# Attention heads in pairs on two halves of the matrix array

## The chip, the cores and the metric

One core of a Trainium2 chip runs the whole program: two transformer layers (a mixer with a dense feed-forward, a mixer with a mixture of experts), and then a third block with a state space branch and a dilated attention branch. The metric is the device time of one execution in microseconds (us). The engines are TensorE (PE: matmuls and transposes; PEld: its weight loads), VectorE (DVE), ScalarE (ACT), GpSimd (POOL) and SyncE (SP, which issues most DMAs).

## What is computed

256 tokens of 1024 features, all in float32. The attention kinds that matter here, with `q`, `k`, `v` per head:

```python
# mixer, per layer: 4 stick-breaking heads (64), 8 latent heads (keys 96, values 64), 4 banded heads (64)
z = einsum('bqhd,bkhd->bhqk', q, k) * scale            # stick-breaking
log_1mb = where(strict, log_sigmoid(-z), 0.0)
tail = lax.cumsum(log_1mb, axis=3, reverse=True) - log_1mb
w = where(strict, exp(log_sigmoid(z) + tail), 0.0)
o = einsum('bhqk,bkhd->bqhd', w, v)
...
p = softmax(where(allowed, s, NEG), axis=-1)            # latent and banded heads
o = einsum('bhqk,bkhd->bqhd', p, v)
...
# third block: 8 heads (64) in 3 groups of dilations 1, 4, 16; the groups of a head share one softmax
o = einsum('gbsh,gbshd->bshd', softmax(stack(lses)), stack(outs))
# and 32 state space heads: y_diag + y_off of ssd_chunked
```

## The kernel before

Large products run in three passes (`mm3`, `lin_feat`): weights and activations are split into a rounded part (`whi`, `hhi`) and a rest (`wlo`, `hlo`), ACT casts and DVE subtracts. The heads' own products are plain fp32.

Everything beside the large products is written as generators, called units, each `yield` ending a step. A large product calls `hook()` after each piece, `hook()` calls `tick()`, and `tick()` moves every active unit by one step, then starts at most one of `pending`, as long as the weights of the active units (1 by default) stay within `cap[0]`. `now(u)` starts a unit at once with weight 0. This gives the order in which instructions are written down. A scheduler then orders each engine's instructions by a simulated timeline: of those that are ready, the one written first goes first. So a unit's instruction may wait for a tile or a bank while later ones pass it. The engines run their queues in the order so made and wait on semaphores.

PSUM tiles come from four tags with few banks: `d` 3, `s` 2 (scores, and transposes of q and k), `t` 1 (transposes of weights to be applied, sums), `o` 2 (accumulators of heads). While `alone[0]` is set, `abank` takes `s` and `d`, or `t` and `d`, in turn.

`softmax_head` (L724 to L756) is one latent or banded head of a mixer: two score products `psc` (L727, L728) into one bank, two reductions with the mask on DVE (L731, L733), two exponentials on ACT, the division on DVE (L743 to L745), three transposes `ppt` (L750), a copy `pT` on ACT (L752), two value products (L755, L756) into the head's half of an accumulator (`om`, `oc`). Between these stand `yield`s. A head of 64 features lies in partitions 0 to 63 or 64 to 127 of its operands by its number; a latent head's 96 features always lie in partitions 0 to 95. Values always fill half of the output's partitions, by the head's number.

`stick_heads` does four heads: scores `pz` (L773, L774), Abs, Exp, Ln on ACT, masks on POOL, a second set of products `pz` (L790 to L792), Exp, and values `os` (L803, L804).

`mixer` announces `band_T`, four latent heads, four banded, four latent; then the stick products q, k, v run, and after them the loop that fills time until the latent heads' norm is done:

```python
        alone[0] = True
        if first:
            ada_rate[0] = 1
        cap[0] = 5
        ...
        now(stick())
        while M.hi[1] is None:
            tick()
            ada_steps(4)
```

`ada_steps(4)` writes down four steps of the adaptive scales (`ada_gen`): products of 1 MB weight tiles with a vector on DVE (L525, L527), summed on PE (`pada`). In the first mixer four scales are outstanding, in the second none.

In the third block (`second`) the dilated heads come as `dil_head` (L1547): three score steps (`pasc`, L1556, L1557, with reductions at L1560), a shared maximum, exponentials, the division, three times transposes `papT` (L1580 to L1582), a copy `apT`, and values `pao` (L1592, L1593). The products of q, k, v are computed in two halves of four heads; a half's heads are announced behind it, so half 0's heads run along with half 1's products (`cap` 2), and half 1's with the first products of the state space branch (`cap` 4). `ssd_group` (state space heads) has its products into `py` at L1723 and L1725.

Of the kernel before, what the change touches and what calls it, by code (L numbers as in the profile page):

```python
# [37 lines left out]
class Split:  # L38
    """An activation, features on partitions: per pair of 128-feature chunks a rounded tile and the rest."""
# [23 lines left out]
def tile_hybrid_stack(ctx: ExitStack, tc: tile.TileContext, a, out, stages=STAGES):  # L63
    nc = tc.nc
    P = 128
# [9 lines left out]
    # tag: (bytes per partition, slots)  # L75
# [64 lines left out]
    # work that feeds later products lets a norm on the way of the next one pass  # L140
# [8 lines left out]
    def tick():  # L149
        """every active unit moves by a step, the oldest first; then at most one starts"""  # L150
# [13 lines left out]
    def now(u):  # L164
        """start a unit at once"""
# [101 lines left out]
    # silu(c), one column per chunk of 128  # L267
# [25 lines left out]
    def rows_of(src, r0, nk, c0, n, tag):  # L293
        """weights in tiles of other use, one per chunk of 128 rows"""
# [30 lines left out]
    def cuts(KC, step):  # L325
        """chunks in steps, an odd piece first"""
# [3 lines left out]
    def reqs(src, KC, c0, n, step):  # L330
        """announces the weights of a product, in the order of their use"""
# [51 lines left out]
    def lin_tok(X, KC, src, c0, n, step=4, order=None, before=None, tag="d"):  # L383
        """tokens on partitions: [128, n] per tile of tokens; order: the first chunks of the weight tiles;
        before: called ahead of the weight tile that starts at a chunk"""
# [7 lines left out]
        for k0 in order:  # L393
# [6 lines left out]
            if X.fresh:  # L400
                # the rests of the activation come a little later than its rounded part
# [21 lines left out]
    def turns(nk, last):  # L423
        """chunk and tile of tokens; the last weight tile completes one tile of tokens ahead of the other"""
# [4 lines left out]
    def lin_down(X, KC, src):  # L429
        """tokens on partitions, 1024 columns, one half after the other: banks [t]"""  # L430
# [12 lines left out]
    def lin_feat(X, KC, src, c0, n, step=4, banks=None):  # L443
        """features on partitions: banks [128, 2, 256], two chunks of 128 features each"""
# [147 lines left out]
    def square_half(t, hf):  # L592
        """mean square of half a row, plus eps and the mean square of the other half if that came first"""
# [30 lines left out]
    def turn_half(t, hf):  # L624
        """half of the columns of x of a tile of tokens, features on partitions"""
# [7 lines left out]
    def turned_x():  # L633
        """x, features on partitions: banks of two chunks"""
# [6 lines left out]
    def norm_split(A, B, tag="p"):  # L641
        """normed x, scaled, features on partitions"""
# [81 lines left out]
    def softmax_head(qT, kT, m0, m1, scale, v, o):  # L724
        """causal in blocks of 128: qT, kT [K, 256], v two [128, 64], o [64, 256] in PSUM"""
        ps = abank((128, 512), "psc", "s")
        mm(ps[:, 0:128], qT[:, 0:128], kT[:, 0:128], start=True, stop=True)  # L727
        mm(ps[:, 128:384], qT[:, 128:256], kT, start=True, stop=True)  # L728
        s = pt([128, 384], name="sc", tag="c")
        mx = small([128, 2], name="mx")  # L730
        vec.tensor_tensor_reduce(out=s[:, 0:128], in0=ps[:, 0:128], in1=m0, scale=scale, scalar=-3e38,  # L731
                                 op0=ALU.add, op1=ALU.max, accum_out=mx[:, 0:1])
# [25 lines left out]
    def stick_heads(q, k, v, o):  # L758
# [12 lines left out]
        for h in range(4):  # L771
# [5 lines left out]
            if h % 2:  # L777
                yield
# [1190 lines left out]
```

## Time and profile before

| | |
|---|---|
| median of 3 runs | 2056.91 us (2054.84 to 2059.88) |
| span of the profiled execution | 2056.6 us |
| PE busy | 97% |
| PE weight loads busy | 85% |
| DVE busy | 79% |
| ACT busy | 62% |
| granted TensorE clock, mean | 0.983 |

The profiled execution is one of its own; its span runs from the first to the last instruction. A matmul's bar in the trace is longer than the time after which the next may start, so the price of a block is read from starts: from the start of the dense matmul ahead of it to that of the one behind. An fp32 product is two matmul instructions in the trace; a form such as `64*128 64x256` means 64 rows and 128 columns of the array, and 256 columns that stream through.

### The profile page before, as it was taken

The page shows a single profiled execution, that of the slowest core. Times are in us where ns is not written, and L with a number is a line of the kernel's source. Part 1 is how long each engine was busy: PE and PEld are TensorE (multiplying, and loading weights), DVE is VectorE, ACT ScalarE, POOL GpSimd, SP SyncE. Part 2 cuts the span into 40 slices and gives each one's busy share as a digit, 9 for nine tenths or more (in the row PEclk, how much of TensorE's full clock was granted, in tenths as well). Part 3 has the DMA queues.
Part 4 walks back from the last instruction along what each step waited for, and adds up shares of the span by engine and source line. Part 5 has one row for each costly group of instructions (what it writes and reads, how often), then busy time and mean ns, then how long its engine had stood idle before and what let it go on. Part 6 is the DMA issues. An engine that isn't in the chain of part 4 may idle for free. (4 is left out here: it accounts for less than half of the span.)

```text
span 2056.6 us, 32577 instructions
## 1 busy us (share of the span) xinstructions
PE 1986.9 (97%) x12095; PEld 1739.1 (85%) x12095; DVE 1634.0 (79%) x2629; ACT 1272.6 (62%) x1962; POOL 128.4 (6%) x207
## 2 busy tenths in 40 slices
PE   6989999998999999999999999989999989999999
PEld 6868998785888888888888888879888889999997
DVE  7888888775699999999999999876667667556784
ACT  2564444455488888788888888755455656545662
POOL 2310000022000000000000000012011010000000
PEclk9998999998899999999999999999999999999999
DMA  9726989662399999999999989845434324555552
GB/s 315 249 91 237 319 306 331 217 191 83 128 335 371 328 372 327 368 326 378 326 376 327 378 313 381 285 145 167 144 104 137 109 84 142 165 185 163 185 165 102
DMA packets 281353, 496.33 MB, mean 241 GB/s; under 512 B 16394, under 2 KB 64852, under 8 KB 281188
## 3 DMA queue, kind: packets, MB, share of 16 engines
q1 hardware_dynamic: 276900, 491.79, 69.0%
q10 hardware_dynamic: 3648, 2.14, 0.4%
q8 instruction: 97, 1.59, 0.3%
q0 software_dynamic: 640, 0.26, 0.1%
q14 instruction: 68, 0.56, 0.1%
HBM read 493.06 MB, written 1.06 MB: 240 GB/s over the span
## 5 line engine op out<-in xcount | busy, mean ns | idle before, releaser
L365 DVE TENSOR_TENSOR wlo<-raw,whi 128x1024 fp32r<-128x1024 f32 (+1 forms) x621 | 749.0, 1218 | 217.7 <-ACT whi L363 210.5
L363 ACT CAST whi<-raw 128x1024 fp32r<-128x1024 f32 (+1 forms) x621 | 647.7, 1048 | 395.2 <-PE pf L475 159.7
L473 PE MATMUL pf<-hhi,whi 128*128 128x256 f32 x1248 | 357.2, 287 | 0.1
L476 PE MATMUL pf<-hhi,wlo 128*128 128x256 f32 x1248 | 356.3, 287 | 0.7 <-DVE wlo L365 0.7
L475 PE MATMUL pf<-hlo,whi 128*128 128x256 f32 x1248 | 356.6, 286 | 0.0
L363 ACT CAST whi<-rawrow 128x512 fp32r<-128x512 f32 x428 | 244.0, 620 | 51.5 <-PE pgu L381 24.9
L365 DVE TENSOR_TENSOR wlo<-rawrow,whi 128x512 fp32r<-128x512 f32 x428 | 270.0, 683 | 0.1
L473 PEld LDWEIGHTS pf<-hhi,whi 128*128 128x128 f32 x1248 | 238.5, 191 | 6.3 <-issue 4.7
L476 PEld LDWEIGHTS pf<-hhi,wlo 128*128 128x128 f32 x1248 | 237.9, 191 | 4.7 <-issue 3.1
L475 PEld LDWEIGHTS pf<-hlo,whi 128*128 128x128 f32 x1248 | 238.6, 191 | 3.3 <-issue 3.0
L380 PE MATMUL pgu<-wlo,xehi 128*128 128x512 f32 (+1 forms) x384 | 144.1, 376 | 0.9 <-DVE wlo L365 0.9
L380 PE MATMUL pgu<-wlo,xehl 128*128 128x512 f32 (+1 forms) x384 | 144.6, 376 | 0.0
L381 PE MATMUL pgu<-whi,xehl 128*128 128x512 f32 (+1 forms) x384 | 142.8, 372 | 0.0
L381 PE MATMUL pgu<-whi,xelo 128*128 128x512 f32 (+1 forms) x384 | 142.7, 372 | 0.0
L379 PE MATMUL pgu<-whi,xehi 128*128 128x512 f32 (+1 forms) x384 | 139.0, 374 | 1.4 <-ACT whi L363 1.4
L379 PE MATMUL pgu<-whi,xehl 128*128 128x512 f32 (+1 forms) x384 | 139.6, 374 | 0.0
L380 PE MATMUL pe<-wlo,ehh 128*128 128x512 f32 x352 | 138.0, 392 | 0.1
L381 PE MATMUL pe<-whi,ehl 128*128 128x512 f32 x352 | 137.1, 389 | 0.0
L379 PE MATMUL pe<-whi,ehh 128*128 128x512 f32 x352 | 136.5, 392 | 0.0
L527 DVE SCALAR_TENSOR_TENSOR acc<-raw,ccol,acc 128x512 f32<-128x512 f32 x164 | 121.7, 747 | 7.4 <-DMA raw<-in_ada_w_dram 5.5
L379 PE MATMUL pt<-whi,hhi 128*128 128x256 f32 (+2 forms) x384 | 115.7, 303 | 0.0
L381 PE MATMUL pt<-whi,hlo 128*128 128x256 f32 (+2 forms) x384 | 114.7, 299 | 0.0
(512 smaller groups left out, 3728.8 us busy)
## 6 DMA issues: line engine op xcount, KB each, us to landing
raw<-in_w_in_dram SPq DMA_DIRECT2D x62, 1024.0 KB
raw<-in_moe_w_up_dram SPq DMA_DIRECT2D x53, 1024.0 KB
raw<-in_moe_w_gate_dram SPq DMA_DIRECT2D x51, 1024.0 KB
raw<-in_moe_w_down_dram SPq DMA_DIRECT2D x45, 1024.0 KB
raw<-in_ada_w_dram SPq DMA_DIRECT2D x44, 1024.0 KB
rawrow<-in_moe_w_gate_dram SPq DMA_DIRECT2D x148, 256.0 KB
rawrow<-in_moe_w_up_dram SPq DMA_DIRECT2D x140, 256.0 KB
rawrow<-in_moe_w_down_dram SPq DMA_DIRECT2D x140, 256.0 KB
```

Source lines behind the costliest of these rows:

```text
L363: behind("hi", nc.scalar.copy(hi[:, i, :], r), 2)
L365: behind("lo", vec.tensor_sub(lo[:, i, :], r, hi.bitcast(F32)[:, i, :]), 2)
L379: mm(ps, lh, wh, start=first, stop=False, skip_group_check=True)
L380: mm(ps, lh, wl, start=False, stop=False, skip_group_check=True)
L381: mm(ps, ll, wh, start=False, stop=last, skip_group_check=True)
L473: mm(o, wh[j][:, s], X.h(kc), start=(kc == 0 and ch % 2 == 0), stop=False, skip_group_check=True)
L475: mm(o, wh[j][:, s], X.l(kc), start=False, stop=False, skip_group_check=True)
L476: mm(o, wl[j][:, s], X.h(kc), start=False, stop=(kc == KC - 1), skip_group_check=True)
L527: behind("ada", vec.scalar_tensor_tensor(acc, raws[k], ccol[:, k:k + 1], acc, op0=ALU.mult, op1=ALU.add))
```

## The change

Two heads that use different halves of the array (rows for scores, columns of the output for values) become one unit of weight 2, and their products are written alternately. `softmax_head` becomes `softmax_pair`, `latent_head` and `band_head` become `latent_heads` and `band_heads`, `dil_head` becomes `dil_heads`. The steps between the products are written head after head, with a `yield` behind each head's. In `stick_heads` and `ssd_group` only the order within two heads changes. The second pair of a half of dilated heads does its transposes and values after the first pair's (`left_of`). All comments are blanked.

```diff
-    def softmax_head(qT, kT, m0, m1, scale, v, o):
+    def softmax_pair(heads, scale):
+        pss = [abank((128, 512), "psc", "s") for _ in heads]
+        for (qT, kT, _, _, _, _), ps in zip(heads, pss):
+            mm(ps[:, 0:128], qT[:, 0:128], kT[:, 0:128], start=True, stop=True)
+        for (qT, kT, _, _, _, _), ps in zip(heads, pss):
+            mm(ps[:, 128:384], qT[:, 128:256], kT, start=True, stop=True)
+        ss, ngs, pTs = [], [], []
+        for (_, _, m0, m1, _, _), ps in zip(heads, pss):
...
+            vec.tensor_scalar_mul(ng, mx, -1.0)
...
+            yield
+        for s, ng in zip(ss, ngs):
...
+            act_exp(s[:, 128:384], s[:, 128:384], AF.Exp, bias=ng[:, 1:2], accum_out=dn[:, 1:2])
+            rd = small([128, 2], name="rd")
+            vec.reciprocal(rd, dn)
...
+            yield
         yield
+        for s in ss:
+            pq = abank((128, 512), "ppt", "t")
...
+            nc.scalar.copy(pT, pq[:, :384])
+            pTs.append(pT)
+            yield
+        obs = [o() for *_, o in heads]
+        for (*_, v, _), pT, ob in zip(heads, pTs, obs):
+            mm(ob, v[0], pT[:, 0:256], start=True, stop=False, skip_group_check=True)
+        for (*_, v, _), pT, ob in zip(heads, pTs, obs):
+            mm(ob[:, 128:256], v[1], pT[:, 256:384], start=False, stop=True, skip_group_check=True)
...
-        for h in range(4):
-            z = abank((128, 512), "pz", "s")
-            mm(z[:, 0:256], k[h][:, 0:128], q[h], start=True, stop=True)
-            mm(z[:, 256:384], k[h][:, 128:256], q[h][:, 128:256], start=True, stop=True)
...
+        for pair in ((0, 1), (2, 3)):
+            bz = [abank((128, 512), "pz", "s") for _ in pair]
+            for h, z in zip(pair, bz):
+                mm(z[:, 0:256], k[h][:, 0:128], q[h], start=True, stop=True)
+            for h, z in zip(pair, bz):
+                mm(z[:, 256:384], k[h][:, 128:256], q[h][:, 128:256], start=True, stop=True)
...
+        for pair in ((0, 1), (2, 3)):
+            obs = [o[h]() for h in pair]
+            for h, ob in zip(pair, obs):
+                mm(ob, v[h][0], head(zs, h)[:, 0:256], start=True, stop=False, skip_group_check=True)
+            for h, ob in zip(pair, obs):
+                mm(ob[:, 128:256], v[h][1], head(zs, h)[:, 256:384], start=False, stop=True, skip_group_check=True)
...
-        lh = [latent_head(h) for h in range(8)]
-        pending.extend([band_T()] + lh[:4] + [band_head(h) for h in range(4)] + lh[4:])
+        lh = [(latent_heads(i), 2) for i in range(4)]
+        pending.extend([band_T()] + lh[:2] + [(band_heads(i), 2) for i in range(2)] + lh[2:])
...
+        def dil_heads(half, i, qT, kT, vt, before):
...
             for g in range(3):
+                pss = [bank(name="pasc", tag="s") for _ in pair]
+                for (hs, *_), ps in zip(pair, pss):
+                    mm(ps[:, 0:128], qT[g][hs, i, 0:128], kT[g][hs, i, 0:128], start=True, stop=True)
+                for (hs, *_), ps in zip(pair, pss):
+                    mm(ps[:, 128:384], qT[g][hs, i, 128:256], kT[g][hs, i, :], start=True, stop=True)
+                for (_, _, mx, at), ps in zip(pair, pss):
...
+                    yield
+            for _, s, mx, _ in pair:
...
+            while before and before[0]:
+                yield
...
+                    if (2 * g + j) % 3 == 2:
+                        vec.tensor_copy(pS, pT[:, :384])
+                    else:
+                        nc.scalar.copy(pS, pT[:, :384])
+                    pTs.append(pS)
+                    yield
...
+                for (hs, *_), hv, pS in zip(pair, vs, pTs):
+                    mm(outs[key][hs, i, :], vt[g][:, 0, hv], pS[:, 0:256], start=(g == 0), stop=False,
+                       skip_group_check=True)
+                for (hs, *_), hv, pS in zip(pair, vs, pTs):
+                    mm(outs[key][hs, i, 128:256], vt[g][:, 1, hv], pS[:, 256:384], start=False, stop=(g == 2),
+                       skip_group_check=True)
+            if i == 0:
+                left_of[half][0] = 0
+                return
...
-            pending.extend(dil_head(half, j, qT, kT, vt) for j in range(4))
+            pending.extend((dil_heads(half, i, qT, kT, vt, left_of[half] if i else None), 2) for i in range(2))
...
-                for h in range(4):
-                    o = py[(h % 2) * 64:(h % 2) * 64 + 64, h // 2, t * P:(t + 1) * P]
-                    mm(o, Xg[t][:, h, :], at[:, t, h * P:(h + 1) * P], start=True, stop=(t == 0))
+                for h2 in range(2):
+                    os = [(h, py[(h % 2) * 64:(h % 2) * 64 + 64, h // 2, t * P:(t + 1) * P])
+                          for h in (2 * h2, 2 * h2 + 1)]
+                    for h, o in os:
+                        mm(o, Xg[t][:, h, :], at[:, t, h * P:(h + 1) * P], start=True, stop=(t == 0))
                     if t == 1:
-                        mm(o, st[:, h, :], ce[:, h, :], start=False, stop=True)
+                        for h, o in os:
+                            mm(o, st[:, h, :], ce[:, h, :], start=False, stop=True)
```

## Rows read from the trace of the kernel before

**Rows 1.** The page: busy us, share of the span, instructions of each engine.

```profile
PE 1986.9 (97%) x12095; PEld 1739.1 (85%) x12095; DVE 1634.0 (79%) x2629; ACT 1272.6 (62%) x1962; POOL 128.4 (6%) x207
```

**Rows 2.** Stretches: length, busy PE, PEld, DVE, ACT, POOL, granted clock, DMA share, GB/s.

```profile
97.60:146.30 48.70, 44.66 (x263) 31.64 (x261) 36.65 (x132) 30.35 (x83) 5.01 (x10) 1.00 0.16 57
146.30:184.30 38.00, 32.66 (x149) 27.69 (x149) 32.38 (x50) 13.65 (x18) 6.05 (x6) 0.82 0.82 280
461.90:510.90 49.00, 43.80 (x237) 29.70 (x236) 27.27 (x114) 30.61 (x83) 11.61 (x28) 0.90 0.25 75
1444.00:1528.30 84.30, 82.47 (x587) 70.73 (x587) 51.67 (x136) 37.62 (x61) 8.37 (x8) 1.00 0.37 113
1552.00:1608.20 56.20, 55.44 (x373) 44.47 (x373) 37.31 (x109) 27.01 (x50) 3.21 (x4) 1.00 0.32 104
```

**Rows 3.** Timeline of PE, one dilated head's scores: start us, us, instruction, count.

```profile
1551.70 0.28 PE L475 MATMUL pf<-hlo,whi 128*128 128x256 f32 x1
1551.82 0.28 PE L476 MATMUL pf<-hhi,wlo 128*128 128x256 f32 x1
1552.03 0.48 PE L1556 MATMUL pasc<-aT,aT 64*128 64x128 f32 x2
...
1552.88 0.38 PE L473 MATMUL pf<-hhi,whi 128*128 128x256 f32 x1
```

**Rows 4.** Timeline of PE, two dilated heads' scores next to each other.

```profile
1569.30 0.28 PE L473 MATMUL pf<-hhi,whi 128*128 128x256 f32 x1
1569.51 0.50 PE L1556 MATMUL pasc<-aT,aT 64*128 64x128 f32 x4
...
1570.38 0.38 PE L475 MATMUL pf<-hlo,whi 128*128 128x256 f32 x1
```

**Rows 5.** Timeline of PE, one dilated head's values.

```profile
1498.36 0.28 PE L379 MATMUL pt<-whi,hhi 128*128 128x256 f32 x1
1498.57 0.65 PE L1592 MATMUL pao<-apT,av 128*64 128x256 f32 x2
...
1499.37 0.39 PE L380 MATMUL pt<-wlo,hhi 128*128 128x256 f32 x1
```

**Rows 6.** Timeline of PE, values of two stick heads, then of a latent head.

```profile
501.49 0.66 PE L803 MATMUL os<-sbz,sbv 128*64 128x256 f32 x4
...
502.19 0.59 PE L755 MATMUL om<-pT,mv 128*64 128x256 f32 x2
...
502.93 0.49 PE L702 MATMUL prb<-ident,rstd 128*128 128x128 f32 x2
```

**Rows 7.** Timeline of PE, a state space group's products, first and second chunk.

```profile
1630.96 0.66 PE L1723 MATMUL py<-at,Xt 128*64 128x128 f32 x8
1631.55 0.39 PE L476 MATMUL pf<-hhi,wlo 128*128 128x256 f32 x1
...
1644.99 0.45 PE L1723 MATMUL py<-at,Xt 128*64 128x128 f32 x4
...
1646.07 0.39 PE L473 MATMUL pf<-hhi,whi 128*128 128x256 f32 x1
```

**Rows 8.** Timeline of DVE, the reductions of two dilated heads' scores.

```profile
1554.19 0.28 DVE L1560 CUSTOM_DVE_ANT_0 ascore<-pasc,dm 128x128 f32<-128x128 f32 x1
...
1555.53 0.28 DVE L1560 CUSTOM_DVE_ANT_0 ascore<-pasc,dm 128x128 f32<-128x128 f32 x1
```

**Rows 9.** Timeline of PE, banded heads' scores in the first mixer.

```profile
112.29 0.50 PE L727 MATMUL psc<-cT,cT 64*128 64x128 f32 x4
```

**Rows 10.** Timelines of DVE and PE at the first mixer's end.

```profile
145.41 4.06 DVE L527 SCALAR_TENSOR_TENSOR acc<-raw,ccol,acc 128x512 f32<-128x512 f32 x6
...
156.18 0.79 PE L379 MATMUL pt<-whi,mhi 128*128 128x512 f32 x1 [1.65 <-ACT mhi L373]
```

**Rows 11.** Stretches in the second mixer: columns as in the second group.

```profile
470.00:475.00 5.00, 3.92 (x16) 2.33 (x17) 4.82 (x28) 3.56 (x15) 0.77 (x2) 0.81 0.00 0
475.00:480.00 5.00, 5.00 (x17) 2.63 (x17) 1.89 (x10) 1.52 (x6) 0.00 (x0) 0.50 0.02 3
```

More of the change, by code (lines that the diff above doesn't have):

```diff
@@ L1031, in latent_pair, with latent_heads @@
             yield
-        def latent_head(h):
-            i, j = h // 2, h % 2
+        def latent_heads(i):
             qh, kh = pairs[i]
             key = "m%d" % (i // 2)
-            yield from softmax_head(qh[0:96, j, :], kh[0:96, j, :], cmask[:, 128:256], cmask, 96 ** -0.5,
-                                    [mv[0][:, h, :], mv[1][:, h, :]], target(key, i % 2, j))
-            if h % 4 == 3:
-                close(key, 1 + h // 4)
+            yield from softmax_pair([(qh[0:96, j, :], kh[0:96, j, :], cmask[:, 128:256], cmask,
+                                      [mv[t][:, 2 * i + j, :] for t in range(2)], target(key, i % 2, j))
+                                     for j in range(2)], 96 ** -0.5)
+            if i % 2:
+                close(key, 1 + i // 2)
         exp_and_ln()
@@ new lines, in dil_heads @@
+        def dil_heads(half, i, qT, kT, vt, before):
+            pair = []
+            for j in range(2):
+                s = pt([128, 1152], name="ascore", tag="d")
+                pair.append((slice(64 * j, 64 * j + 64), s, small([128, 6], name="amx"),
+                             [(s[:, 128 * g:128 * g + 128], s[:, 384 + 256 * g:640 + 256 * g]) for g in range(3)]))
+            for g in range(3):
+                pss = [bank(name="pasc", tag="s") for _ in pair]
[4 more added lines that the diff above has]
+                for (_, _, mx, at), ps in zip(pair, pss):
+                    for b, (p_, m) in enumerate(((ps[:, 0:128], dm[0][:, g, :]), (ps[:, 128:384], dm[1][:, g, :]))):
+                        vec.tensor_tensor_reduce(out=at[g][b], in0=p_, in1=m, scale=1.0, scalar=-3e38, op0=ALU.add,
+                                                 op1=ALU.max, accum_out=mx[:, 3 * b + g:3 * b + g + 1])
+                    yield
+            for _, s, mx, _ in pair:
+                ng = small([128, 2], name="ang")
+                vec.tensor_reduce(ng, mx.rearrange("p (b g) -> p b g", g=3), axis=AX.X, op=ALU.max)
+                vec.tensor_scalar_mul(ng, ng, -1.0)
+                yield
+                dn = small([128, 2], name="adn")
+                parts = (s[:, 0:384], s[:, 384:1152])
+                for b in range(2):
+                    act(parts[b], parts[b], AF.Exp, bias=ng[:, b:b + 1], accum_out=dn[:, b:b + 1])
+                yield
+                vec.reciprocal(dn, dn)
+                for b in range(2):
+                    vec.tensor_scalar(parts[b], parts[b], dn[:, b:b + 1], None, op0=ALU.mult)
+                yield
+            while before and before[0]:
+                yield
@@ L1588, in dil_head @@
-                yield
+                pTs = []
+                for j, (_, _, _, at) in enumerate(pair):
+                    pT = bank(name="papT", tag="t")
+                    nc.tensor.transpose(pT[:, 0:128], at[g][0], ident)
+                    nc.tensor.transpose(pT[:, 128:256], at[g][1][:, 0:128], ident)
+                    nc.tensor.transpose(pT[:, 256:384], at[g][1][:, 128:256], ident)
+                    pS = pt([128, 384], name="apT", tag="m")
+                    if (2 * g + j) % 3 == 2:
[3 more added lines that the diff above has]
+                    pTs.append(pS)
+                    yield
@@ L1589, in dil_head @@
                 if key not in outs:
                     outs[key] = bank((128, 2, 256), "pao", "o")
[L1591 to L1600 removed]
+                vs = [slice((2 * i + j) * 64, (2 * i + j) * 64 + 64) for j in range(2)]
@@ L1603, in second @@
+            f = pt([128, 2, 256], name="aof")
+            vec.tensor_copy(f, outs.pop(key))
+            h_, l_ = split(f, [128, 2, 256], "ao", "e")
+            AT.hi.append(h_)
+            AT.lo.append(l_)
+        left_of = [[1], [1]]
         cw = [cols["cw"][:, 32 * k:32 * k + 32] for k in range(4)]
```

118 lines of the change are left out of this document (27 added, 91 removed).

## The prediction

> **What bounds the kernel now.** The page comes first: TensorE (PE) is busy for 97% of the span, VectorE (DVE) for 79%, ScalarE (ACT) for 62% [rows 1]. A busy PE is a bad measure of a full one, so the second view is the table by stretches, cut at the five places where attention heads run, and at the stretch after the first mixer [rows 2]. In the two stretches of the dilated heads (the fourth and fifth rows) PE is busy for 82.47 of 84.30 us and for 55.44 of 56.20 us, DVE for about two thirds, and the DMA engines for a third: there every us of PE time counts. The chain that ended last agrees: through these stretches nearly all of its pieces are PE's. In the mixers' attention (first and third rows) PE is busy for 44.66 of 48.70 and 43.80 of 49.00 us, but no dense product runs beside the heads, so PE, DVE (36.65) and ACT (30.35) hand work to each other, and a us less on one of them is not a us less in time. The third view is the timeline of PE around single blocks; it gives the prices.
>
> A head's fp32 product stands there as two instructions each. A dense matmul starts every 0.12 us; one dilated head's scores push the next dense one from 1551.82 to 1552.88, so they cost 1.06 - 0.12 = 0.94 us [rows 3]. One head's values cost 1499.37 - 1498.36 - 0.12 = 0.89 us [rows 5].
>
> **What the change does to each price.** The trace of before already holds what the change wants, by accident. At 1569.51 us two heads, one in rows 0 to 63 of the array and one in rows 64 to 127, have their scores next to each other: eight instructions instead of four, and dense work goes on after 1570.38 - 1569.30 = 1.08 us [rows 4]. That is 0.02 us more than for one head, so the second head is free: a pair saves 0.92 us. For values, where the heads differ in the output's columns, two stick heads take from 501.49 to 502.19 = 0.70 us, one latent head right behind them 502.93 - 502.19 = 0.74 us [rows 6]. Again the second head is free: 0.89 us saved per pair where it stands among dense products, 0.74 us in the mixers.
>
> A rule of the Trainium skill speaks against the values' half: the page "TensorE: Matmul & The Clock Gate", Part 3, The mechanism, says that weight loads overlap matmuls in flight only when the row group differs, and two heads' values have the same 128 rows. By it the values would save nothing and the whole change 7.7 us in place of the 20.4 us below; the trace disagrees with the rule [rows 6], and the row decides.
>
> Now the sum, place by place.
>
> Dilated values: 8 heads in 3 groups make 12 pairs; 12 x 0.89 = 10.7 us at most, 0 at least, if a pair's products do not get next to each other. In the new code the two products stand together behind both transposes, with a piece of dense product between these, so both copies should be in by then. I take eight tenths: 8.5 us.
>
> Dilated scores: 12 pairs, of which one overlaps already [rows 4]: 11 x 0.92 = 10.1 us at most, 0 at least. Here the second head can come late. A pair takes both score banks, and a bank comes back when DVE has reduced it; in the trace the two heads' reductions start at 1554.19 and 1555.53, 1.34 us apart [rows 8], while one head's scores occupy PE only from 1552.03 to 1552.88, 0.85 us [rows 3]. If the first head's products go as soon as its bank is free, they are over before the second's may start. Against it: a piece of dense work stands between two steps of a pair and is issued first. I take six tenths: 6.1 us.
>
> Mixers: 8 latent and 4 band heads per layer make 12 pairs of values, 12 x 0.74 = 8.9. Stick values are 4 pairs, about half of it already overlapped as in rows 6: 1.5. Band scores are 4 pairs, of which one in each mixer overlaps already [rows 9]: 2 x 0.92 = 1.8. Stick scores are 4 pairs, one overlapped already: 3 x 0.74 = 2.2. Latent scores use rows 0 to 95 for both heads, so nothing. The most is 14.4 us. The least is 0, because DVE and ACT set the pace as often as PE. PE idles there for 48.70 - 44.66 = 4.0 us already [rows 2], and part of what is saved becomes more of that. I take four tenths, 2.9 us in each mixer: 5.8 us.
>
> State space heads: nothing. Their eight instructions of the first chunk alternate halves today and take 1631.55 - 1630.96 = 0.59 us; the sixteen of the second take 1646.07 - 1644.99 = 1.08 us, so they run two abreast too [rows 7].
>
> Switching the array between whole and half costs about 0.2 us per block and is inside these differences; a pair switches once where two heads switched twice. Transposes, copies, exponentials and reductions are the same in number and size, so DVE and ACT lose and gain nothing. Their order changes: head two of a pair trails head one by a step. The wait of the second pair for the first (`left_of`) delays nothing that I can find: by my count of steps half 0's pairs need 37 of the 52 places that half 1's products offer, and half 1's pairs end at about the 25th, where the state space work is only just announced.
>
> Sum: 8.5 + 6.1 + 5.8 = 20.4 us. The profiled span is 2056.6 us and the median of the runs 2056.9 us (the table of times), so 0.3 us lies between them: 2056.9 - 20.4 = 2036.5 us. With every fraction at one it would be 2056.9 - 10.7 - 10.1 - 14.4 = 2021.7 us.
>
> **The rivals.**
> *Pairs that don't meet, or that free time nobody needs.* Scores stagger as above, and the values of half 1 fill a hole: near its end almost no dense product runs, so a shorter block there may only lengthen a wait. For it: rows 8; the mixers' idle time. Against it: PE is over 97% busy in both dilated stretches [rows 2]. Keeping a third of each term (35.2 / 3 = 11.7) it gives 2045, keeping a tenth 2053: about 2049 us.
> *Only scores gain.* If two heads in different columns did not run abreast, the values' terms would go, and 6.1 and the mixers' score terms, (1.8 + 2.2) x 0.4 = 1.6, stay: 2056.9 - 7.7 = 2049.2 us. Against it stand the stick values [rows 6] and the state space blocks [rows 7], both in halves of columns. This is the rule on weight loads of the Trainium skill's page named above, as far as it goes for values.
> *Slower: the first mixer's last heads go behind the adaptive scales.* Once the dense products are through, each bare `tick()` issues `ada_steps(4)`. By my count the last latent head is through after 5 such ticks today; with pairs, that weigh 2 under a cap of 5 and take 8 steps, after 13. So 8 x 4 = 32 more steps, some 28 of them DVE instructions, come before the last pair in program order. One costs 4.06 / 6 = 0.68 us [rows 10]: 19 us of DVE work. DVE idles for 48.70 - 36.65 = 12.05 us in that stretch [rows 2], which hides part. The same steps ask for the fourth scale's 4.2 MB ahead of the output weights, 15 us at the 280 GB/s of the second row. The output product, which starts at 156.18 us [rows 10], waits for these heads' norm. So the price is between 19 - 12 = 7 and 19 + 15 = 34 us. Against it: this work is needed before the feed-forward anyway, and DVE works on it alone from 145.41 us while PE waits; issued earlier it may shorten that. It must exceed the other gains, 8.5 + 6.1 + 2.9 = 17.5 us, to decide; at 26 us the time is 2056.9 - 17.5 + 26 = 2065 us.
> *The clock*, as a smaller cost inside the ranges: in the second mixer the granted clock falls to 0.50, the lower of its two levels (1.2 GHz), in 475 to 480 us, after five us in which PE was busy for 3.92 [rows 11]. PE work takes twice as long there: these five us cost 2.5 us, the partial drop before them (0.81) 1 us, and about as much follows. Pairs make PE idle more, so the first mixer could pay these 5 us too, or the second be spared.
>
> **How the numbers follow.** Forecast (12 to 35 us gained): 0.55. Pairs that don't meet: 0.20, half of it within 0.3%. Only scores: 0.05. Slower: 0.20, of which 0.03 ends within 0.3% and 0.17 beyond. A difference under 0.3%, 6 us, can't be told from none. Faster: 0.55 + 0.10 + 0.05 = 0.70; same: 0.10 + 0.03 = 0.13; slower: 0.17. The predicted time is the forecast's. The range goes from below the full sum, 2018, to 2059, which takes in the first two rivals and the mild end of the third, and leaves out some 0.15 above and 0.03 below. The forecast's own range is 2021.7 to 2045.
>
> **What the profile after would show.** Right: in the dilated stretches, blocks of eight score and eight value instructions, followed by dense work after about 1.1 and 1.0 us; the stretch from the first dilated scores to the last values shorter by 12 to 18 us; both mixers shorter by 1 to 6 us; state space blocks as before. A step is wrong if score blocks stay in fours with dense matmuls between them (fraction of scores), if eight instructions of values take 1.6 us (columns don't overlap), if DVE's scale work stands ahead of the last latent pair and the output product of the first mixer starts later than now (the slower rival), or if the second mixer's clock stays whole or the first's falls (some 5 us either way without any of my reasons).

## Result, and the profile after the change

The changed kernel takes 2079.14 us (median of 4 runs, 2073.28 to 2081.08) against 2055.88 us for the kernel before beside it: a ratio of 1.0106, 95% interval 1.0088 to 1.0124. It is slower by some 22 us, where 20 us of gain were forecast. The profiled execution has a span of 2078.5 us, so it can be compared with the 2056.6 us of before. The page of the changed kernel, its busy line and the granted clock in 40 slices:

```profile
PE 1995.4 (96%) x12095; PEld 1741.6 (84%) x12095; DVE 1638.8 (79%) x2629; ACT 1272.2 (61%) x1962; POOL 131.4 (6%) x207
...
PEclk9987999999799999999999999999999989999999
```

The instructions are the same in number as in [rows 1]; PE is busy 8.5 us longer for them, and the span is 21.9 us longer. So PE did not get less to do, and it waits and runs at the lower clock more (mean granted clock 0.973 in place of 0.983). Where, a table of stages tells. A stage is counted from the first transpose of x for one norm (tile `ptr`) to that of the next, in the trace of each kernel (us; the kernels below the second are experiments, told further down):

| kernel | first mixer | feed-forward | second mixer | experts | third block | rest |
|---|---|---|---|---|---|---|
| before | 175.8 | 180.4 | 175.0 | 816.0 | 495.1 | 205.8 |
| after | 192.3 | 178.8 | 180.9 | 818.3 | 495.2 | 204.6 |
| dil_only | 175.9 | 179.8 | 170.2 | 815.6 | 496.9 | 205.0 |
| mix_only | 191.9 | 179.4 | 175.4 | 818.5 | 498.6 | 204.7 |
| dil_adjv | 175.9 | 179.8 | 170.2 | 816.0 | 490.0 | 204.8 |
| dil_adjvs | 175.3 | 180.4 | 175.1 | 815.7 | 483.1 | 205.0 |
| after_ada2 | 184.0 | 182.3 | 178.8 | 818.2 | 495.1 | 204.6 |
| before_ada7 | 187.7 | 177.3 | 172.9 | 815.6 | 495.1 | 204.4 |
| after_w1 | 170.3 | 180.7 | 169.6 | 818.7 | 495.1 | 204.6 |
| after_w1_ada8 | 189.9 | 179.7 | 165.8 | 819.7 | 495.7 | 204.8 |
| best_w1 | 169.5 | 181.4 | 170.6 | 818.4 | 484.3 | 204.8 |

The third block, where 14.6 us of gain were forecast, has its old length. The first mixer alone loses 16.5 us.

**The dilated pairs did not meet.** The timeline of PE in the changed kernel, values of one pair (L1620 the 256 columns, L1623 the 128):

```profile
1504.38 0.27 PE L1608 MATMUL papT<-ident,ascore 128*128 128x128 f32 x1
1504.58 0.65 PE L1620 MATMUL pao<-apT,av 128*64 128x256 f32 x2
1505.16 0.39 PE L379 MATMUL pt<-whi,hhi 128*128 128x256 f32 x1
...
1507.65 0.28 PE L381 MATMUL pt<-whi,hlo 128*128 128x256 f32 x1
1507.86 0.43 PE L1620 MATMUL pao<-apT,av 128*64 128x256 f32 x1
1507.87 0.43 PE L1623 MATMUL pao<-apT,av 128*64 128x128 f32 x2
1508.13 0.38 PE L1620 MATMUL pao<-apT,av 128*64 128x256 f32 x1
1508.34 0.38 PE L1623 MATMUL pao<-apT,av 128*64 128x128 f32 x2
1508.65 0.33 PE L1606 MATMUL papT<-ident,ascore 128*128 128x128 f32 x1
```

The first head's product of 256 columns goes alone at 1504.58; then come dense products, and 3.3 us later the other head's, with both products of 128 columns. The copies on ACT, which these products wait for:

```profile
1503.31 0.47 ACT L1613 COPY apT<-papT 128x384 f32<-128x384 f32 x1
1504.69 0.48 ACT L1613 COPY apT<-papT 128x384 f32<-128x384 f32 x1 [0.91 <-PE papT L1608]
```

The second copy has ended by 1505.17, 2.7 us ahead of its product, so this product did not wait for its copy. Its place in PE's queue was fixed when the program was built, by the scheduler's simulated timeline; that the first product was ready there when the second was not is what I read from this order. That pair costs 1505.16 - 1504.38 = 0.78 us and 1508.65 - 1507.65 = 1.00 us, less 0.11 us each for the instruction ahead, 1.56 us in all; two single heads cost 2 x 0.89 = 1.78 us [rows 5]. Nine of the twelve pairs look like this. The last three stand in one piece, but without dense work between their instructions, and take 1.4 to 1.8 us, since PE waits inside them for the copies.

Scores, the same view (L1576 and L1578):

```profile
1585.29 0.28 PE L475 MATMUL pf<-hlo,whi 128*128 128x256 f32 x1
1585.50 0.49 PE L1576 MATMUL pasc<-aT,aT 64*128 64x128 f32 x2
1585.82 0.59 PE L1578 MATMUL pasc<-aT,aT 64*128 64x256 f32 x2
1586.35 0.38 PE L476 MATMUL pf<-hhi,wlo 128*128 128x256 f32 x1
```

Four instructions and then dense work again, for 1.06 us from dense to dense, exactly as in [rows 3]. The second head's products follow at 1588.33 us, although DVE had reduced what the two score banks held before by 1585.48 us (L1581): in this pair, too, it is the place in the queue that keeps PE from going on. Of twelve pairs of scores one stands as eight instructions (at 1467.76 us); one did so before, too [rows 4].

**The first mixer.** The view by stretches, columns as in [rows 2], cut at the last latent head's values (plus 0.7 us) and at the first output product. First the kernel before, then the changed one:

```profile
97.60:143.70 46.10, 42.05 (x247) 29.73 (x245) 34.61 (x127) 29.55 (x82) 4.80 (x10) 1.00 0.14 47
143.70:156.18 12.48, 7.14 (x41) 6.01 (x40) 11.92 (x22) 4.52 (x7) 3.52 (x3) 0.71 0.72 261
156.18:184.30 28.12, 28.12 (x124) 23.59 (x125) 22.50 (x33) 9.93 (x13) 2.73 (x4) 0.89 0.85 286
```

```profile
97.60:159.70 62.10, 51.59 (x285) 37.24 (x284) 49.99 (x155) 30.17 (x83) 7.21 (x12) 0.81 0.37 119
159.70:177.70 18.00, 13.16 (x52) 10.95 (x52) 15.54 (x26) 6.39 (x9) 1.89 (x2) 0.59 0.88 298
177.70:200.70 23.00, 23.00 (x99) 18.89 (x99) 11.82 (x14) 7.91 (x10) 0.59 (x1) 0.95 0.59 198
```

The heads end 16.0 us later, the output product starts another 5.5 us later, and 5.1 us come back in it, where DVE has 11.82 us of work in place of 22.50 and the clock is at 0.95 in place of 0.89. In the first row of after DVE has 49.99 us of work in place of 34.61, and the clock is at 0.81 in place of 1.00; PE's bars are 9.5 us longer, though only 38 instructions more lie in the stretch. DVE's additional work is the adaptive scales. The same view for their line alone (L527; DVE busy, count) up to the first output product, before and after:

```profile
97.60:156.18 58.58, 15.22 (x21) 0.94 0.26 92
```

```profile
97.60:177.70 80.10, 30.90 (x42) 0.76 0.48 159
```

What 42 instead of 21 of them do at the end, the timelines of DVE, PE and ACT in the changed kernel show. `pss`, `gss`, `prb` are the last latent heads' norm; `pada` belongs to the scales:

```profile
164.56 3.52 DVE L527 SCALAR_TENSOR_TENSOR acc<-raw,ccol,acc 128x512 f32<-128x512 f32 x5
168.00 0.15 DVE L696 COPY gss<-pss 128x2 f32<-128x2 f32 x1
168.12 3.11 DVE L527 SCALAR_TENSOR_TENSOR acc<-raw,ccol,acc 128x512 f32<-128x512 f32 x4
173.01 2.36 DVE L365 TENSOR_TENSOR wlo<-raw,whi 128x1024 fp32r<-128x1024 f32 x2 [1.78 <-ACT whi L363]
175.29 1.65 DVE L706 SCALAR_TENSOR_TENSOR gfull<-oT,cols,prb 128x256 f32<-128x256 f32 x4
```

```profile
164.40 3.54 PE L693 MATMUL pss<-ones,sq 128*128 128x1 f32 x16 [0.95 <-DVE adac L543]
168.21 2.08 PE L534 MATMUL pada<-acc,ones 128*128 128x512 f32 x2 [0.27 <-DVE gss L696]
170.08 1.92 PE L536 MATMUL pada<-ident,cols 128*128 128x128 f32 x8
171.78 1.06 PE L702 MATMUL prb<-ident,rstd 128*128 128x128 f32 x4
```

```profile
171.94 2.94 ACT L363 CAST whi<-raw 128x1024 fp32r<-128x1024 f32 x3 [8.67 <-DMA raw<-in_w_out_dram]
```

The norm's small copy (0.15 us) stands behind five scale instructions on DVE, its spreading over partitions (`prb`) behind ten products of the scales on PE, and the output weights, requested at 162.16 us behind eight requests of the scales' weights, are first cast at 171.94 us (before: requested at 142.96, cast at 147.96). The weights end last: the norm's last step on DVE (`gfull`, L706) stands behind their splits (L365). All three belong to the rival that ended slower.

### The profile page after: what moved, and what is told of

It reads as the page before. It is cut to its first block, busy times and chain, and to the rows that moved or that the text cites. A ratio compares the mean times of both kernels' runs of the same rounds, so it can differ in the third digit from the quotient of the medians.

```text
span 2078.5 us, 32573 instructions
## 1 busy us (share of the span) xinstructions
PE 1995.4 (96%) x12095; PEld 1741.6 (84%) x12095; DVE 1638.8 (79%) x2629; ACT 1272.2 (61%) x1962; POOL 131.4 (6%) x207
## 3 DMA queue, kind: packets, MB, share of 16 engines
HBM read 493.06 MB, written 1.06 MB: 238 GB/s over the span
## 5 line engine op out<-in xcount | busy, mean ns | idle before, releaser
L365 DVE TENSOR_TENSOR wlo<-raw,whi 128x1024 fp32r<-128x1024 f32 (+1 forms) x621 | 749.0, 1218 | 231.9 <-ACT whi L363 223.8
L365 DVE TENSOR_TENSOR wlo<-rawrow,whi 128x512 fp32r<-128x512 f32 x428 | 270.2, 685 | 0.1
L381 PE MATMUL pgu<-whi,xehl 128*128 128x512 f32 (+1 forms) x384 | 142.8, 372 | 0.0
L527 DVE SCALAR_TENSOR_TENSOR acc<-raw,ccol,acc 128x512 f32<-128x512 f32 x164 | 121.3, 749 | 6.8 <-DMA raw<-in_ada_w_dram 4.5
L380 PE MATMUL pt<-wlo,hhi 128*128 128x256 f32 (+2 forms) x384 | 115.6, 301 | 0.4 <-DVE wlo L365 0.4
```

The costliest lines, as they stand in the source:

```text
L365: behind("lo", vec.tensor_sub(lo[:, i, :], r, hi.bitcast(F32)[:, i, :]), 2)
L380: mm(ps, lh, wl, start=False, stop=False, skip_group_check=True)
L381: mm(ps, ll, wh, start=False, stop=last, skip_group_check=True)
L527: behind("ada", vec.scalar_tensor_tensor(acc, raws[k], ccol[:, k:k + 1], acc, op0=ALU.mult, op1=ALU.add))
```

## The experiments

Each run was timed beside the kernel before, which took 2054.7 to 2057.9 us in the different sessions; so the ratios are compared and not the medians.

| kernel | median us | ratio to before | 95% interval |
|---|---|---|---|
| dil_only | 2055.27 | 0.9993 | 0.9983 to 1.0004 |
| mix_only | 2078.55 | 1.0104 | 1.0088 to 1.0120 |
| dil_adjv | 2049.65 | 0.9965 | 0.9952 to 0.9977 |
| dil_adjvs | 2043.68 | 0.9938 | 0.9924 to 0.9951 |
| stick_adjv | 2050.05 | 0.9976 | 0.9966 to 0.9985 |
| after_ada2 | 2073.39 | 1.0079 | 1.0065 to 1.0093 |
| before_ada7 | 2063.22 | 1.0035 | 1.0022 to 1.0049 |
| after_w1 | 2050.22 | 0.9974 | 0.9962 to 0.9986 |
| after_w1_ada8 | 2065.63 | 1.0049 | 1.0034 to 1.0065 |
| before_cap | 2056.21 | 1.0010 | 1.0001 to 1.0020 |
| before_two | 2073.25 | 1.0084 | 1.0068 to 1.0100 |
| best_w1 | 2037.75 | 0.9916 | 0.9902 to 0.9929 |
| best_w1_mval | 2038.89 | 0.9920 | 0.9907 to 0.9934 |
| best_w1_ada2 | 2041.52 | 0.9929 | 0.9916 to 0.9943 |

A difference of two ratios times 2056 us gives the us below.

**The two halves of the change, each alone.** dil_only has the functions of before for the mixers; mix_only has `dil_head` and the old order in `ssd_group`.

```diff
-        lh = [(latent_heads(i), 2) for i in range(4)]
+        lh = [latent_head(h) for h in range(8)]        # dil_only
...
-            pending.extend((dil_heads(half, i, qT, kT, vt, left_of[half] if i else None), 2) for i in range(2))
+            pending.extend(dil_head(half, j, qT, kT, vt) for j in range(4))        # mix_only
```

> Dilated pairs and the new order in the state space groups, with both mixers as before. My theory from the two traces (the loss is all in the mixers, and the dilated pairs hardly meet): the third block keeps its length, so 2054 to 2058 us, no difference that can be told. The rival, my forecast's terms for the dilated heads (8.5 + 6.1 us), which the mixers would only have hidden in the sum: 2042 us. A second rival, that the new order costs in the third block by itself: over 2062 us.

> Pairs in both mixers (softmax pairs and stick order), dilated and state space heads as before. Theory: the whole loss is here, 16 us in the first mixer and 4 us in the second, so 2075 to 2080 us. Rival: the loss comes from how the two parts follow each other (the weights' requests or the clock further down), then each part alone costs less than the whole and this run stands below 2068 us.

Both as the theory says: 0.9993 and 1.0104. The dilated pairs and the state space order change nothing that can be told; the mixers carry all of the loss.

**Values that meet.** In dil_adjv the later head's product is written first and the other held behind it on PE.

```diff
-                for (hs, *_), hv, pS in zip(pair, vs, pTs):
-                    mm(outs[key][hs, i, :], vt[g][:, 0, hv], pS[:, 0:256], start=(g == 0), stop=False,
...
+                last = None
+                for (hs, *_), hv, pS in list(zip(pair, vs, pTs))[::-1]:
+                    op = mm(outs[key][hs, i, :], vt[g][:, 0, hv], pS[:, 0:256], start=(g == 0), stop=False,
...
+                    if last is not None:
+                        after(op, last)
+                    last = op
```

> As dilated pairs alone, but the late head's first value product is written first and the other's is held behind it, so that all twelve pairs of values stand as eight instructions next to each other. Theory: a pair then takes PE 0.9 us where the split one takes 0.58 + 0.80 = 1.37 us, so 12 x 0.5 = 6 us of PE time are saved, and as the stretch is 97% PE the time is 4 to 6 us below that of dilated pairs alone. Rival (values end in a hole that absorbs it): blocks of eight with 0.9 us, but within 2 us of dilated pairs alone.

0.9965 against 0.9993: 5.8 us, and the third block 6.9 us shorter (490.0 against 496.9). The timeline of PE in this run:

```profile
1476.61 0.28 PE L476 MATMUL pf<-hhi,wlo 128*128 128x256 f32 x1
1476.82 0.65 PE L1601 MATMUL pao<-apT,av 128*64 128x256 f32 x4
1477.30 0.39 PE L1607 MATMUL pao<-apT,av 128*64 128x128 f32 x4
1477.62 0.33 PE L1586 MATMUL papT<-ident,ascore 128*128 128x128 f32 x1
```

Eight instructions in 1477.62 - 1476.61 - 0.12 = 0.89 us, which is what one head cost alone [rows 5]: the second head is free. The Trainium skill's page "TensorE: Matmul & The Clock Gate", Part 3, The mechanism, says that weight loads overlap matmuls in flight only where row groups differ; these heads use the same rows and different columns, and the second line above, where the second head costs nothing with the same rows, disagrees with it.

**Scores that meet.** The pair's two banks come from different tags, and the later product is written first, as above.

```diff
-                pss = [bank(name="pasc", tag="s") for _ in pair]
+                pss = [bank(name="pasc", tag=k) for k in "sd"]
```

> Mixers as before; dilated pairs with their values next to each other, and their scores too: the second head's bank is taken from the dense products' three, and the later product is written first. 9 or 10 of the 12 score groups then stand as eight instructions. Theory (scores too are worth 0.9 us per pair as soon as they meet): 7 to 9 us below the run with adjacent values alone, about 2041 us. Rival (the bank is missing in the dense products, or the reductions follow too late): within 2 us of it or slower.

0.9938 against 0.9965: 5.6 us, a little less than expected. The third block is 6.9 us shorter again. By the trace eight of the twelve pairs meet; one of them:

```profile
1547.49 0.28 PE L475 MATMUL pf<-hlo,whi 128*128 128x256 f32 x1
1547.70 0.49 PE L1557 MATMUL pasc<-aT,aT 64*128 64x128 f32 x4
1548.02 0.60 PE L1562 MATMUL pasc<-aT,aT 64*128 64x256 f32 x4
1548.56 0.38 PE L476 MATMUL pf<-hhi,wlo 128*128 128x256 f32 x1
```

1.07 us from dense to dense for two heads, as in [rows 4]. Bank and order were changed together, so the run does not tell which of the two had made the scheduler keep the scores apart.

**The stick order.** dil_adjv with the new `stick_heads`.

> The run with adjacent dilated values, and the stick heads of both mixers in the new order of pairs; latent and banded heads single as before. Theory (the mixers' loss comes from the softmax pairs alone): within 3 us of the run with adjacent dilated values, about 2050 us. Rival (the stick order takes its part of the loss): over 2055 us.

0.9976 against 0.9965, with intervals that overlap: no part of the loss, and no gain either. As mix_only shows the whole loss, the softmax pairs carry it.

**The scale steps.** The number of steps per bare tick, in both directions.

```diff
         while M.hi[1] is None:
             tick()
-            ada_steps(4)
+            ada_steps(2)        # after_ada2; before_ada7 has 7 in the kernel before
```

> The changed kernel with two steps of the adaptive scales per bare tick in place of four: 16 ticks write down 32 steps ahead of the output product (36 before, 64 with the change). Theory (the scale steps stand ahead of the last latent pairs and of the output product): the first output product goes back from 177.7 to about 160 to 165 us, and the time from 2079 to 2062 to 2068 us. Rival (the pairs themselves are late, since the last latent pairs start later and take more steps, and the clock falls with the idle time): the first output product stays behind 170 us and the time above 2073 us.

> The kernel before with seven steps of the adaptive scales per bare tick in place of four, nothing else: 9 ticks write down 63 steps ahead of the output product (36 before, 64 with the change), with single heads as before. Theory (the steps by themselves are about half of the first mixer's loss, as halving them gave back 8 us of its 16): the first mixer 6 to 10 us longer, of which the feed-forward behind it gives back 2 to 4, so 2061 to 2065 us. Rival (the steps only fill time in which the last pairs are late anyway): within 2 us of the kernel before.

after_ada2 fell between the two: 1.0079, that is 5.6 us back of 21.8 (the two intervals touch; by the profiles the first two stages together are 4.8 us shorter), with the output product at 166.9 us. The stretches of its first mixer, cut as above:

```profile
97.60:154.50 56.90, 46.75 (x266) 32.68 (x262) 40.88 (x136) 32.23 (x86) 6.95 (x12) 0.88 0.28 93
154.50:166.90 12.40, 8.34 (x39) 7.92 (x38) 9.98 (x21) 2.35 (x4) 0.89 (x2) 0.55 0.52 170
166.90:192.40 25.50, 25.50 (x104) 20.99 (x105) 16.04 (x21) 8.28 (x11) 0.80 (x2) 0.88 0.69 236
```

The middle stretch is back at before's length (12.40 against 12.48), and the output weights are cast at 143.77 us. But the heads' stretch is still 56.90 - 46.10 = 10.8 us longer, and the scales don't account for it: up to the output product 23 instructions of L527 run (21 before), 14 of them in the first stretch (10 before), some 3.3 us more. before_ada7 came out at the expected time, 7.2 us slower, with single heads, though its first mixer is 11.9 us longer, where 6 to 10 were expected:

```profile
97.60:147.70 50.10, 44.25 (x261) 31.30 (x261) 39.64 (x136) 29.75 (x82) 5.79 (x10) 1.00 0.18 64
147.70:166.20 18.50, 9.00 (x41) 8.42 (x40) 16.70 (x32) 2.33 (x5) 1.89 (x2) 0.52 0.99 345
166.20:196.10 29.90, 29.86 (x129) 24.03 (x130) 21.59 (x28) 12.91 (x17) 1.78 (x4) 0.90 0.81 279
```

Its middle stretch has the 18 us of the changed kernel, its first one only 4.0 us more than before. So the steps make the middle stretch long, and something else makes the heads late. What that is, the scores show. The second score products (`psc`) of the latent heads in the first mixer, the times being the first and the last start; before, after, and after_w1, which follows below:

```profile
L728 PE MATMUL psc<-mT,mT x16: 379/380/382, 103.7 to 130.5; 96*128 96x256 f32 x16
L731 PE MATMUL psc<-mT,mT x16: 379/380/634, 103.9 to 138.3; 96*128 96x256 f32 x16
L731 PE MATMUL psc<-mT,mT x16: 380/382/637, 103.2 to 123.3; 96*128 96x256 f32 x16
```

The last one starts at 130.5 us before and at 130.3 in before_ada7, at 138.3 us after and at 138.9 in after_ada2. So the pairs of weight 2 have their last scores 8 us later, whatever the number of steps. The steps lengthen what follows, from these scores to the end of the heads' stretch: 13.2 us before, 17.4 in before_ada7, 21.4 after, 15.6 in after_ada2.

**The weight.** A pair weighs 1 in place of 2, the caps stay, so the third and fourth latent pairs start earlier in the order in which instructions are written down. The loop then makes 8 rounds in place of 16, so it also writes down 32 scale steps in place of 64.

```diff
-        lh = [(latent_heads(i), 2) for i in range(4)]
-        pending.extend([band_T()] + lh[:2] + [(band_heads(i), 2) for i in range(2)] + lh[2:])
+        lh = [latent_heads(i) for i in range(4)]
+        pending.extend([band_T()] + lh[:2] + [band_heads(i) for i in range(2)] + lh[2:])
```

> The changed kernel, but a pair of the mixers weighs 1 instead of 2 under the same caps, so latent pairs 2 and 3 start earlier: the last latent pair is through after 4 bare ticks (12 with the change, 5 before) and the loop ends after 8 (16 and 9). Theory (the weight holds the last pairs back, and the scale steps of each tick go ahead of them): the first output product goes back from 177.7 to 152 to 160 us, the time to 2050 to 2058 us. Rival (pairs are slow whatever their start, because two heads hold twice the banks and wait for each other): the first output product stays behind 168 us and the time above 2068 us.

> Pairs of weight 1 with eight steps of the adaptive scales per bare tick: 32 steps are written down by the time the last latent pair is through and 64 by the end of the loop (16 and 32 with four steps, 48 and 64 with the change). Theory (scale steps ahead of the output product cost 6 to 9 us whatever the heads do): 2056 to 2060 us. Rival (steps cost only where the last pairs are late): within 2 us of pairs of weight 1, 2048 to 2052 us.

after_w1 is 27 us faster than the changed kernel (0.9974 against 1.0106) and 5.3 us faster than before. Its first mixer:

```profile
97.60:135.90 38.30, 36.08 (x200) 23.56 (x199) 27.58 (x117) 25.72 (x78) 2.56 (x4) 0.96 0.09 29
135.90:149.10 13.20, 10.26 (x77) 8.56 (x76) 12.95 (x24) 6.49 (x10) 5.28 (x8) 0.99 0.57 191
149.10:178.80 29.70, 29.18 (x132) 24.57 (x133) 24.87 (x36) 10.43 (x14) 2.38 (x3) 0.89 0.89 320
```

The last latent scores start at 123.3 us. The heads' stretch is 23.8 us shorter than in the changed kernel, 7.8 us shorter than before. after_w1_ada8 was underestimated: 1.0049, or 15.4 us more than with four steps, where 6 to 9 were expected. With early heads the 32 more steps have no late head behind which to hide; with late ones (1.0106 less 1.0079) they cost 5.6 us. That they hide there is my reading of the two differences; no run shows it by itself. The four kernels with pairs tell the two causes apart: weight 1 in place of 2 is worth 21.6 us with 32 steps in the loop (1.0079 to 0.9974) and 11.7 us with 64 (1.0106 to 1.0049); 32 steps in place of 64 are worth 5.6 us with weight 2 and 15.4 us with weight 1.

**Early start or meeting?** Two runs asked whether after_w1's gain over the kernel before needs pairs at all: single heads, with caps of 8 and 10, and then with up to two starts per tick as well.

```diff
-        if pending:
+        for _ in range(starts[0]):        # 2 in the mixers, before_two; before_cap has only the caps
+            if pending:
...
-        cap[0] = 5
+        cap[0] = 10
```

> The kernel before with single heads everywhere, but the mixers' caps raised from 4 and 5 to 8 and 10 once the heads are announced: as many heads may be under way as with pairs of weight 1. Theory (the gain of the pairs of weight 1 over the kernel before, some 4 us in the mixers, comes from the early start, not from pairing): 2047 to 2051 us. Rival (it comes from products that meet on the array): 2053 to 2058 us, no difference that can be told.

> The kernel before with single heads, caps of 8 and 10 as in the run with raised caps, and up to two heads started per tick in the mixers, so that single heads start as early as pairs of weight 1 do. Theory (the gain of pairs of weight 1 in the mixers is the early start): the last latent values in the first mixer start at 134 to 138 us, the time is 2048 to 2052 us. Rival (it is products that meet): the heads start early but the time stays at 2053 to 2058 us.

before_cap gains nothing (1.0010), but its last latent values start at 142.8 us against 143.0: with one start per tick the caps were not what held the heads, so the run tells nothing. In before_two the heads do start early, with the last latent scores at 121.7 us, but the last latent values start at 140.5 us, not at 134 to 138, and the time is 17 us longer: the first mixer takes 183.6 us, the feed-forward 187.4 and the second mixer 180.6, which is 7.8, 7.0 and 5.6 us more than before. Five of the scales' DVE instructions (L529 there) lie ahead of the output product in place of 21, so the shorter loop wrote down fewer steps, and that work falls behind it; how much of the 17 us this is, no run shows. Neither theory nor rival fits. So an early start of single heads brought nothing here, and whether after_w1 gains over the kernel before by pairs or by the early start stays open.

**Both parts mended.** best_w1 is after_w1 with the dilated values and scores of dil_adjvs; best_w1_mval also holds the mixers' value pairs together; best_w1_ada2 has two scale steps per tick.

> Pairs of weight 1 in the mixers, and dilated pairs whose values and scores both meet. Theory (the two gains add, since they stand in different stages): 2037 to 2041 us. Rival (they share a limit further down): above 2043 us.

> As the run before it in this list, and the values of the latent and banded pairs are held together in the same way (the late head's product first). Theory (my forecast's four tenths of what meets, 12 pairs x 0.5 us x 0.4): 2 to 3 us below it. Rival (in the mixers PE waits for DVE and ACT, so nothing): within 1.5 us of it.

> Pairs of weight 1, dilated values and scores that meet, and two scale steps per bare tick instead of four. Theory (with the heads early, every step ahead of the output product still costs, as 64 steps cost 15 us more than 32): 2 to 6 us below the run with four steps. Rival (with 32 steps the first output product no longer waits for them, and what is left out must be done later anyway): within 2 us of it or slower, since the feed-forward then waits for its scales.

best_w1 is the fastest: 0.9916, some 17 us below the kernel before. The gains add. Of the twelve pairs of latent and banded values in the two mixers two stand as eight instructions in best_w1 and all twelve in best_w1_mval; that brings nothing (0.9920), so PE's time in these products is not what the mixers wait for. Fewer steps shorten the first mixer by 3.7 us more and lengthen the feed-forward by 7.4 us (188.8 against 181.4). In its first 25.7 us PE is busy for 20.59 us at a clock of 0.73, against 22.88 us at 0.93 in best_w1, and it waits for 2.1 us for the scales' sums (`pada`, L541): the rival's way.

## Why the prediction was wrong, step by step

- **Price of a pair: right.** Two heads in halves of rows or of columns cost what one costs (0.89 us for values, 0.95 us for scores), by [rows 4] and [rows 6] and by dil_adjv and dil_adjvs. That also rules out the rival by which only scores gain.
- **Dilated values, 8.5 us: wrong step "both copies should be in by then".** Writing two products next to each other does not put them next to each other in PE's queue. Each is placed when the simulated timeline has its own copy ready, which is a transpose and a copy later for the second head, and dense work goes between. None of the nine pairs beside dense work met. Held together, they gave 5.8 us, about what their rows say: a split pair costs 1.56 us and a whole one 0.89, and 9 x 0.67 = 6.0 us.
- **Dilated scores, 6.1 us: the same fault.** "A piece of dense work stands between two steps of a pair" did not bring them together; [rows 8] had shown the 1.34 us between the two banks, and the counterargument was given too much. One of twelve met. With a bank of another tag and the order held, eight met and gave 5.6 us.
- **Mixers, 5.8 us gain: wrong sign, and wrong in its reason.** As changed, the mixers lose 21 us. The pairs of weight 1 gain about 4.5 us (0.9938 to 0.9916, intervals that overlap), which is near the term by luck: the term stood mostly for values that meet, ten of twelve pairs of latent and banded values do not meet in best_w1, and where all do (best_w1_mval) nothing more is gained.
- **The slower rival: right in its mechanism, too low in its chance, and only half the story.** 21 more L527 instructions lie ahead of the output product (28 DVE instructions were forecast), 15.7 us of DVE time (19 forecast), the output weights come late, and its time, 2065, is 14 us too low. It counted the eight additional ticks only for the steps that they write down. The weight of 2 under a cap of 5 also makes the last two pairs start later: by 8 us at their scores, and by some 7 to 11 us in the heads' stretch of after_ada2 (10.8, less the 3.3 of scale work if none of it is hidden). The second mixer has no steps at all and points the same way, though its length differs by some 5 us between runs with the same mixers: 175.4 to 180.9 us in three runs with weight 2, 170.2 to 175.2 us in six with single heads as before (180.6 in before_two), 165.8 to 170.6 us in five with weight 1.
- **State space heads nothing: right** (dil_only). **Stick heads:** no gain to be told.
- **The second pair waits for the first at no cost: right, by luck.** The last dilated values start 251.8 us into the third block before (1607.5 - 1355.7) and 273.5 us after (1652.2 - 1378.7), so the count of places missed a delay; the runs do not tell how much of it the wait makes and how much the pairs' weight. The block's length did not change all the same.
- **The clock: as feared, size open.** The first mixer's heads run at 0.81 in place of 1.00, the middle stretch at 0.59 in place of 0.71. How much of the heads' delay is the clock and how much waiting, no run separates. Open, too, is a loss of 2.3 us among the experts, which all runs with softmax pairs show (818.2 to 820.0 against 815.6 to 816.0 us), and before_two as well.

The two dilated terms, where the products are held together, give 5.8 + 5.6 = 11.4 us against 14.6, and the mixers' term gives nothing by products that meet. So the step that failed was not a price but the belief that the change brings the products together and leaves the heads' starts alone: it brought none of nine value pairs and one of twelve score pairs together, and it put the last latent scores of the first mixer 8 us later.

## What to carry to other kernels

A scheduler that places what is ready keeps no two products together because they are written together: hold the one that is ready first behind the one that is ready last, and make sure that the second's buffer can be free at that time. When units are merged, read their weight, caps and steps again: a merged unit that weighs double starts later, and everything written down per tick in the longer loop moves ahead of it. Background work per tick is a balance: too many steps delay the heads' norm, too few the next layer.

## What the runs showed of the hardware

The granted clock in one stretch differed between two profiled executions whose kernels have the same code there. In the second mixer, from 475 to 480 us, it was 0.50 before [rows 11]. In dil_adjv, whose mixers are unchanged and run at the same times within a us, the same stretch has it at 1.00:

```profile
475.00:480.00 5.00, 4.38 (x30) 2.79 (x29) 3.23 (x19) 2.67 (x9) 3.00 (x7) 1.00 0.03 7
```

In the five us ahead PE was busy for 3.92 us before and for 4.18 us in dil_adjv, and in the five ahead of those for 4.16 us in both. The stage takes 175.0 and 170.2 us, and with the same mixers again 170.2 us in dil_only and 175.1 us in dil_adjvs. So one profiled execution can't tell a gain of 5 us in such a stretch; the timed rounds can.
